# Hybrid attention block: weighted sums moved into the PSUM buffer of the step before, a narrower sum, and row sums by a column of ones

## The chip, the cores and the metric

The kernel runs on 1 core of one Trainium2 chip. The metric is the time on the device in microseconds (us). A run's time is that of one execution, and several runs are given by their median.

## The reference

One encoder layer over L = 16 meta tokens + 1024 frames of width 1024. RMSNorm, one input projection, two groups of eight heads, each head gated by a SiLU path, an output projection, RMSNorm and the residual. Cut to what matters here:

```python
for q0 in range(0, L, Q_BLOCK):                      # 128 queries at a time
    kend = key_end(q0)
    s = einsum('bqhd,bkhd->bhqk', q[:, q0:q0+Q_BLOCK], k[:, :kend]) * scale
    s = mask_and_bias(s, q0, kend)                   # causal + decay (FoX), chunk-causal (MLA)
    p = softmax(s, axis=-1)
    outs.append(einsum('bhqk,bkhd->bqhd', p, v[:, :kend]))
fox = ... * silu(f_gate); mla = ... * silu(m_gate)
y = concat([fox, mla]) @ w_out
return x + rmsnorm_post(y)
```

The head width is 64 in both groups. All products run in pairs of fp16 parts (a high part, and the rest as a low part), so that one product of the reference is three on the chip: high with high, high with low, low with high.

## The kernel before

**Stages.** A first stage normalises and transposes x and makes the latents and the values. Then come 16 heads, first 8 FoX heads and then 8 MLA heads, each of four steps; a tail finishes the output projection. A step treats a pair of query tiles, (7, 0), (6, 1), (5, 2) or (4, 3), so each step has nine key blocks of 128 and two short ones of 16 meta tokens: 1,184 columns of scores.

**One step n** (`step`):
- TensorE (PE): the scores of both tiles go into a PSUM buffer `sc` of three banks; there are two such buffers, used in turn. `places` leaves its first 256 columns free.
- VectorE (DVE): `peaks` takes two row maxima from PSUM, and one small operation makes the biases `nbs` (L806, L808).
- ScalarE (ACT): two exponentials from PSUM into `pr`, in f32 (L890). Each also sums its rows by `accum_out`, which costs a second instruction, the read of the accumulator.
- ACT writes the high fp16 part `ph` (L821); DVE subtracts to get the low part (L825), GpSimd (POOL) the part of the meta tokens (L902). This second half is emitted in the next step.
- A DMA transposes `ph` into `pT` (L905), which SyncE (SP) issues.
- Three steps after its scores (LAG = 3) a pair's weighted sums run on PE (`weighted`, L833 and L834), and DVE adds their two halves into `onat` (L918). They use the 256 free columns of the buffer that the step just then filled with its own scores.

`weighted` holds `pT` as the stationary operand, one load of weights for each product. The moving operand is `Vt`, whose high and low parts lie side by side: one product of 128 columns for the high part of the probabilities (11 in a step), one of 64 for their low part (9 in a step). The output of a tile is 128 columns wide.

**What orders the rest.** Between the steps `work` emits pieces of jobs: projections of the next heads (L960 to L962, L1174 to L1176, L1192 to L1194), and from the MLA heads on parts of the output projection (L1259 to L1261). Their results go through two one-bank buffers of `ps_g`. The framework tracks dependencies by PSUM bank and reorders each engine's instructions when the kernel is built, by when it expects them to be ready, so an engine's order in the trace need not be that of the code. On the chip each engine runs its own in that order.

**After a head.** `head_end` divides a head's rows by their sums (a reciprocal on DVE, a product on POOL); the last head does so pair by pair in `tiles_end`. In the tail the last three weighted sums use the third bank of the buffers that hold the output projection, `spare`.

Of the kernel before, what the change touches and what calls it, by code (L numbers as in the profile page):

```python
# [10 lines left out]
F32 = mybir.dt.float32  # L11
# [37 lines left out]
def hybrid_kernel(ctx, tc, x, meta, norm_pre, norm_post, w_in, b_f, q_norm, w_uq, kv_norm, w_ukv, w_out,  # L49
# [71 lines left out]
    Vt = V_pool.tile([P, NT + 1, H + 1, 2, HD], F16, name="Vt")  # L121
# [308 lines left out]
    def latents_V(t):  # L430
# [6 lines left out]
        split_v(pv, scale_mu, vm[:, :, 0, :], vm[:, :, 1, :])  # L437
        SY.dma_start(vm_d[:, :, t].rearrange("h p k d -> p h k d"), vm)

    def values_out(t, ps):  # L440
        split_v(ps, scale_fu, Vt[:, t, 1 : H + 1, 0, :], Vt[:, t, 1 : H + 1, 1, :])
# [333 lines left out]
    AVW = 2 * 2 * HD  # L775
# [60 lines left out]
    def head_end(onat, hh, sums):  # L836

        rs = at.tile([P, NT], F32, name="rs", tag="rs", bufs=2)
        V.reciprocal(rs, sums)
        o = onat[:, :, hh * HD : (hh + 1) * HD]  # L840
        G.tensor_tensor(o, o, rs.unsqueeze(2).to_broadcast([P, NT, HD]), ALU.mult)
# [31 lines left out]
    steps = {}  # L873

    def step(first, av=None):
# [3 lines left out]
        if first is not None:  # L879
            (ia, ib), passes, mask, mask_w, inv, sums = first[0:6]  # L880
            ps = step_psum("sc")
            av = ps[:, 0:AVW]
# [3 lines left out]
            pr = at.tile([P, wa + wb], F32, name="pr", tag="pr", bufs=2)  # L886
            prs = pr[:, 0:wa], pr[:, wa : wa + wb]
            for i, x, nb, p in reversed(list(zip((ia, ib), sc, nbs, prs))):

                A.activation(p, x, AF.Exp, bias=nb, scale=inv, accum_out=sums[:, i : i + 1])  # L890
# [3 lines left out]
            steps[n] = dict(t=(ia, ib), pr=prs, prw=pr, ph=ph, phs=(ph, ph[:, B0 * P :]), los=los, rest=first[6:])  # L894
# [17 lines left out]
        if old is not None:  # L912
            (ia, ib), pT = old["t"], old["pT"]
            vh, onat, hh, after = old["rest"]
            avs = av.rearrange("p (i t d) -> p i t d", i=2, t=2)
            weighted(avs[:, 1], ia, pT, pT[:, B0 + ib + 2 :, :], vh)
            weighted(avs[:, 0], ib, pT[:, B0:, :], pT[:, ia + 2 :, :], vh)
            V.tensor_reduce(onat[:, ib : ia + 1 : ia - ib, hh * HD : (hh + 1) * HD], avs.rearrange("p i t d -> p i d t"),  # L918
                            AX.X, ALU.add)
            if after is not None:  # L920
                after(ia, ib)

    def run_head(head, vh, hh, passes, mask, mask_w, inv, onat, after, each=None):

        sums = at.tile([P, NT], F32, name="sums", tag="sums", bufs=2)

        def end(ia, ib):
            head_end(onat, hh, sums)
# [4 lines left out]
        if each is not None:  # L933
            ends = [lambda ia, ib: each(ia, ib, sums)] * len(STEPS)

        total = sum(j[1] for j in jobs if j[0] == head)
        for k, tiles in enumerate(STEPS):
            step((tiles, passes, mask, mask_w, inv, sums, vh, onat, hh, ends[k]))
# [27 lines left out]
    def decays():  # L966
# [6 lines left out]
        V.tensor_tensor_scan(ncum[:, 0:NM], ones8f[0:H].to_broadcast([H, NM]), pf[0:H, 112:128], 0.0, ALU.mult, ALU.subtract)  # L973
        for t in range(1, NT + 1):
            T.transpose(pf[0:H, 512 + (t - 1) * P : 512 + t * P], lu[:, t, :], ident)
        V.tensor_tensor_scan(ncum[:, NM:L], ones8f[0:H].to_broadcast([H, S]), pf[0:H, 512:], ncum[:, NM - 1 : NM], ALU.mult, ALU.subtract)
# [243 lines left out]
    def load_values(h):  # L1220

        SY.dma_start(Vt[:, :, h], vm_d[h])
# [93 lines left out]
    ended = []  # L1316

    def tiles_end(ia, ib, sums):
        both = slice(ib, ia + 1, ia - ib)
        rs = at.tile([P, 2], F32, name="rs2", tag="rs2", bufs=2)  # L1320
        V.reciprocal(rs, sums[:, both])
        o = onat[:, both, HD:P]
# [180 lines left out]
```

## Time and profile before

| what | value |
| --- | --- |
| three runs | 628.46, 631.99, 632.98 us, median 631.99 |
| the profiled execution's own time | 630.43 us |
| its span | 628.6 us |
| mean granted clock of TensorE | 0.982 of full speed |
| PE busy | 558.2 us, 89% of the span |
| DVE busy | 478.2 us, 76% |
| ACT busy | 416.5 us, 66% |
| POOL busy | 198.8 us, 32% |

Matmuls are pipelined and the profile models their ends, so a busy PE need not be at its peak. "PEld" is the load of weights into TensorE, which runs beside the matmuls. "SPq" is SyncE's queue, from which the DMAs are issued. An idle time of an engine is put down to the instruction that ended it.

### The profile page before, as it was taken

How to read it: one execution, taken by the hardware profiler on the slowest of the kernel's cores; microseconds unless marked ns; L12 is line 12 of the kernel's file. 1: busy time of each engine (PE TensorE's matmuls, PEld its weight loads, DVE VectorE, ACT ScalarE, POOL GpSimd, SP SyncE). 2: the span in 40 equal slices, each digit the busy share in tenths (PEclk: the TensorE clock that was granted, in tenths of full speed). 3: DMA queues.
4: the chain of work that ended last, by engine and by line, in shares of the span. 5: the costliest groups of instructions: out<-in, count | busy, mean ns of one | idle time of the engine just before them, and what ended most of it. 6: DMA issues, size and time to landing. Idle time of an engine off the chain costs nothing.

```text
span 628.6 us, 11590 instructions
## 1 busy us (share of the span) xinstructions
PE 558.2 (89%) x4210; PEld 332.7 (53%) x4210; DVE 478.2 (76%) x953; ACT 416.5 (66%) x820; POOL 198.8 (32%) x282
## 2 busy tenths in 40 slices
PE   2999798989789999999999996988989989998994
PEld 1445354546346565656565553555555655655442
DVE  3778875576858787777797767889988887778667
ACT  5688868456867686656667657678677777686322
POOL 2223333373313233323343222123232313332242
PEclk9999899999999999999999998999999999999998
DMA  8858668165685987594858796697978868897943
GB/s 298 208 135 222 147 178 209 33 179 164 118 184 98 216 179 152 88 235 87 202 101 191 111 206 143 128 170 144 181 170 160 145 158 160 174 225 171 321 173 119
DMA packets 269529, 105.04 MB, mean 167 GB/s; under 512 B 234832, under 2 KB 257360, under 8 KB 269472
## 3 DMA queue, kind: packets, MB, share of 16 engines
q1 hardware_dynamic: 269472, 104.30, 73.5%
q8 instruction: 33, 0.54, 0.3%
q14 instruction: 24, 0.20, 0.1%
HBM read 48.38 MB, written 13.96 MB: 99 GB/s over the span
## 4 chain that ended last, share of the span: by engine, by line
DVE 31%; PE 27%; ACT 22%; issue 10%; DMA 5%; SPq 2%; POOL 1%; ACTq 0%; DVEq 0%; POOLq 0%
ACT pr L890 12%; DVE nb L806 9%; DVE ph L825 5%; ACT ph L821 4%; PE sc L834 3%; PE sc L796 2%; PE ps L306 2%; PE ps L304 2%; PE ps L305 2%; PE psf L1261 2%; PE psf L1259 2%; PE psf L1260 2%; DVE st L1053 2%; DMA wr<-in_w_in 2%; DMA wqr<-in_w_uq 1%
## 5 line engine op out<-in xcount | busy, mean ns | idle before, releaser
L825 DVE TENSOR_TENSOR ph<-pr,ph 128x128 f16<-128x128 f32 (+7 forms) x128 | 98.3, 778 | 30.8 <-ACT ph L821 30.2
L902 POOL TENSOR_TENSOR ph<-pr,ph 128x32 f16<-128x32 f32 x64 | 51.3, 802 | 222.1 <-issue 103.8
L806 DVE TENSOR_REDUCE nb<-sc 128x1 f32<-128x1040 f32 (+7 forms) x128 | 93.1, 766 | 5.6 <-PE sc L799 5.0
L890 ACT ACTIVATE pr<-sc,nbs,fox_inv 128x144 f32<-128x144 f32 (+3 forms) x64 | 53.5, 839 | 46.5 <-DVE nbs L808 41.4
L834 PE MATMUL sc<-Vt,pT 128*128 128x128 f16 x671 | 64.8, 222 | 20.2 <-ACT pr L890 19.4
L796 PE MATMUL sc<-st,st 128*128 128x256 f16 (+5 forms) x496 | 77.0, 291 | 2.2 <-ACT pr L890 1.3
L821 ACT CAST ph<-pr 128x912 f16<-128x912 f32 (+6 forms) x112 | 77.6, 737 | 0.2
L796 PEld LDWEIGHTS <-st 128*128 128x128 f16 x640 | 55.6, 98 | 29.7 <-issue 4.8
L833 PEld LDWEIGHTS <-pT 128*128 128x128 f16 x576 | 51.1, 99 | 35.1 <-issue 34.1
L890 ACT ACTIVATE pr<-sc,nbs,ism 128x144 f32<-128x144 f32 (+3 forms) x64 | 53.5, 840 | 24.3 <-DVE nbs L808 21.8
L834 PEld LDWEIGHTS <-pT 128*128 128x128 f16 x704 | 59.7, 99 | 6.1 <-issue 0.9
L833 PE MATMUL sc<-Vt,pT 128*128 128x64 f16 x549 | 57.9, 195 | 0.0
L960 PEld LDWEIGHTS <-wp 128*128 128x128 f16 x320 | 31.5, 98 | 30.1 <-DVE st L1054 4.9
L961 PEld LDWEIGHTS <-wp 128*128 128x128 f16 x320 | 31.5, 98 | 24.0 <-issue 4.1
L962 PEld LDWEIGHTS <-wp 128*128 128x128 f16 x320 | 31.5, 98 | 23.3 <-issue 0.8
L960 PE MATMUL psq<-xAh,wp 128*128 128x264 f16 x128 | 35.5, 277 | 1.0 <-DVE st L1054 1.0
L961 PE MATMUL psq<-xAl,wp 128*128 128x264 f16 x128 | 35.3, 276 | 0.0
L962 PE MATMUL psq<-xAh,wp 128*128 128x264 f16 x128 | 35.3, 276 | 0.0
L150 DVE SCALAR_TENSOR_TENSOR wp<-wr,bsc,wp 128x1024 f16<-128x1024 f32 x21 | 28.9, 1377 | 1.1 <-ACT wp L149 0.9
L960 PE MATMUL psg<-xBh,wp 128*128 128x512 f16 x64 | 25.1, 392 | 3.7 <-DVE kl L1201 3.2
L960 PE MATMUL psg<-xAh,wp 128*128 128x512 f16 x64 | 24.3, 379 | 2.8 <-DVE st L1054 2.8
L1259 PE MATMUL psf<-wo,xBh 128*128 128x512 f16 (+1 forms) x68 | 24.9, 366 | 1.1 <-DVE onatm L918 0.8
(370 smaller groups left out, 1466.7 us busy)
## 6 DMA issues: line engine op xcount, KB each, us to landing
wr<-in_w_in SPq DMA_DIRECT2D x20, 512.0 KB, 4.8
wr<-in_w_in SPq DMA_DIRECT2D x26, 256.0 KB, 3.9
wor<-in_w_out SPq DMA_DIRECT2D x8, 512.0 KB, 4.4
xr<-in_x SPq DMA_DIRECT2D x8, 512.0 KB, 5.7
xt<-in_x SPq DMA_DIRECT2D x7, 512.0 KB, 4.1
y_d<-ys SPq DMA_DIRECT2D x12, 256.0 KB, 2.3
y<-y_d SPq DMA_DIRECT2D x6, 512.0 KB
out<-y SPq DMA_DIRECT2D x5, 512.0 KB, 2.6
```

What stands on the lines that cost most here:

```text
L796: T.matmul(sc[:, o:o1], sta[:, i * P : (i + 1) * P], mov[:, o - c0 : o1 - c0], start=q == 0, stop=q == len(passes) - 1 and not last)
L806: V.tensor_reduce(nb[:, k : k + 1], part, AX.X, ALU.max, negate=True)
L821: A.copy(ph[:, 112 : 112 + W], pr)
L825: V.tensor_tensor(lo, pr[:, NM:W], ph[:, P : P + W - NM], ALU.subtract)
L833: T.matmul(avf[:, 0:HD], lo[:, j - 1, :], Vt[:, j, vh, 0], start=False, stop=False)
L834: T.matmul(avf, hi[:, j, :], Vt[:, j, vh].rearrange("p t d -> p (t d)"), start=j == 0, stop=j == n)
L890: A.activation(p, x, AF.Exp, bias=nb, scale=inv, accum_out=sums[:, i : i + 1])
L902: G.tensor_tensor(ph[:, 0 : B0 + 1 : B0, 96:112], n1[:, 0 : w0 + 1 : w0, :], ph[:, 0 : B0 + 1 : B0, 112:128], ALU.subtract)
L960: T.matmul(ps[:, 0:n], hi[:, c, :], xT(0, c, c0, n), start=c == 0, stop=False)
L961: T.matmul(ps[:, 0:n], hi[:, c, :], xT(1, c, c0, n), start=False, stop=False)
L962: T.matmul(ps[:, 0:n], lo[:, c, :], xT(0, c, c0, n), start=False, stop=c == NC - 1)
L1259: T.matmul(ps, hi, wh, start=c == first, stop=False)
```

## The change

1. The weighted sums of step n-3 are emitted right behind the scores of step n, and write the first 130 columns of the buffer `sc` of step n-1 (`older_step`, with `last`), no longer that of step n.
2. `Vt` gets rows of 130: low part (64), high part (64), two columns of ones. Each tile's sum is 65 columns wide: high and low probabilities times [high values | ones], 65 columns each (20 in a step), and high probabilities times low values, 64 columns (11 in a step). All add into the same 65 columns.
3. The column of ones gives the row sums, so the exponentials lose `accum_out`.
4. The DVE operation that added the two halves goes. ACT copies the 130 columns from PSUM to a new f32 tile `ona`; this copy is emitted between the step's two exponentials.
5. `head_end` and `tiles_end` read `ona` and write `onat`.
6. In the tail the last three sums use a buffer of `ps_g`; the Square root's table is loaded one step earlier; two transposes of a chain precede both products; a third step buffer takes the place of `spare` for the last tile; two f32 rows come from the pool `fw`.
7. In `decays` the eight transposes precede the first scan.

The diff, cut to its core:

```diff
-    Vt = V_pool.tile([P, NT + 1, H + 1, 2, HD], F16, name="Vt")
+    Vt = V_pool.tile([P, NT + 1, H + 1, 2 * HD + 2], F16, name="Vt")
+    G.memset(Vt[:, :, :, 2 * HD :], 1.0)
...
-        avf = av.rearrange("p t d -> p (t d)")
         for j in range(n + 1):
+            vl, v1 = Vt[:, j, vh, 0:HD], Vt[:, j, vh, HD : 2 * HD + 1]
+            T.matmul(av, hi[:, j, :], v1, start=j == 0, stop=False)
             if j > 0:
-                T.matmul(avf[:, 0:HD], lo[:, j - 1, :], Vt[:, j, vh, 0], start=False, stop=False)
-            T.matmul(avf, hi[:, j, :], Vt[:, j, vh].rearrange("p t d -> p (t d)"), start=j == 0, stop=j == n)
+                T.matmul(av, lo[:, j - 1, :], v1, start=False, stop=False)
+            T.matmul(av[:, 0:HD], hi[:, j, :], vl, start=False, stop=j == n)
...
+    def older_step(n, ps):
+        old = steps.get(n - LAG)
+        if old is None:
+            return
+        (ia, ib), pT = old["t"], old["pT"]
+        vh, ona, after = old["rest"]
+        av = ps[:, 0 : 2 * (HD + 1)].rearrange("p (i d) -> p i d", i=2)
+        weighted(av[:, 1], ia, pT, pT[:, B0 + ib + 2 :, :], vh)
+        weighted(av[:, 0], ib, pT[:, B0:, :], pT[:, ia + 2 :, :], vh)
+        A.copy(ona[:, ib : ia + 1 : ia - ib, :], av)
...
-            ps = step_psum("sc")
-            av = ps[:, 0:AVW]
+            last, psc[0] = psc[0], step_psum("sc")
+            ps = psc[0]
...
-                A.activation(p, x, AF.Exp, bias=nb, scale=inv, accum_out=sums[:, i : i + 1])
+            A.activation(prs[1], sc[1], AF.Exp, bias=nbs[1], scale=inv)
+            older_step(n, last)
+            A.activation(prs[0], sc[0], AF.Exp, bias=nbs[0], scale=inv)
...
+        else:
+            older_step(n, product("av"))
...
-            avs = av.rearrange("p (i t d) -> p i t d", i=2, t=2)
-            weighted(avs[:, 1], ia, pT, pT[:, B0 + ib + 2 :, :], vh)
-            weighted(avs[:, 0], ib, pT[:, B0:, :], pT[:, ia + 2 :, :], vh)
-            V.tensor_reduce(onat[:, ib : ia + 1 : ia - ib, hh * HD : (hh + 1) * HD], avs.rearrange("p i t d -> p i d t"),
-                            AX.X, ALU.add)
...
-        V.reciprocal(rs, sums)
+        V.reciprocal(rs, ona[:, :, HD])
...
-        SY.dma_start(Vt[:, :, h], vm_d[h])
+        SY.dma_start(Vt[:, :, h, 0 : 2 * HD], vm_d[h].rearrange("p t k d -> p t (k d)"))
...
-                            (spare[0][:, 0:256], 768, 256)]
+                            (step_psum("psf")[:, 0:256], 768, 256)]
```

## Rows read from the trace of the kernel before

**Rows 1.** Busy time by stage: the FoX heads, the MLA heads.

```profile
core 0: us, PE busy (x) PEld busy (x) DVE busy (x) ACT busy (x) POOL busy (x), PEclk, DMA share, GB/s
...
156.00:402.00 246.00, 223.04 (x1766) 138.21 (x1765) 183.99 (x316) 163.49 (x307) 71.89 (x92) 0.98 0.75 154
402.00:575.00 173.00, 155.86 (x1455) 98.60 (x1454) 149.09 (x279) 130.86 (x260) 52.32 (x54) 1.00 0.82 162
```

**Rows 2.** PE's waits, 156 to 402, then 402 to 575 us: total, times, longest.

```profile
PE sc L834 <- ACT pr L890: 12.5, 23, 2.9
...
PE sc L834 <- ACT pr L890: 6.8, 15, 1.2
...
PE psf L834 <- DVE onatm L918: 0.8, 1, 0.8
```

**Rows 3.** ACT, then PE, in one step of FoX: timeline (start, duration).

```profile
256.78 1.10 ACT L890 ACTIVATE pr<-sc,nbs,fox_inv 128x912 f32<-128x912 f32 x1
257.77 0.19 ACT L890 ACTIVATION_READ_ACCUMULATOR pr<-sc,nbs,fox_inv 128x1 f32 x1
...
258.02 0.22 PE L834 MATMUL sc<-Vt,pT 128*128 128x128 f16 x1 [0.74 <-ACT pr L890]
258.07 0.19 PE L833 MATMUL sc<-Vt,pT 128*128 128x64 f16 x1
258.10 0.22 PE L834 MATMUL sc<-Vt,pT 128*128 128x128 f16 x1
...
258.89 0.28 PE L961 MATMUL psq<-xAl,wp 128*128 128x264 f16 x1
```

**Rows 4.** Groups by line: busy us, mean ns, idle before.

```profile
L834 PEld LDWEIGHTS <-pT 128*128 128x128 f16 x704 | 59.7, 99 | 6.1 <-issue 0.9 <-DMA st<-lat_d 0.3
L918 DVE TENSOR_REDUCE onat<-sc 128x128 f32<-128x256 f32 x32 | 13.5, 421 | 8.2 <-PE sc L834 8.0
L890 ACT ACTIVATION_READ_ACCUMULATOR pr<-sc,nbs,ism 128x1 f32 x64 | 12.5, 196 | 0.0
```

**Rows 5.** Eight one-column products, each with a load of weights: PE timeline.

```profile
556.38 0.34 PE L1123 MATMUL wosum<-wo_sq,ones 128*128 128x1 bf16 x8
556.58 0.38 PE L1259 MATMUL psy<-wo,ogF 128*128 128x512 f16 x1
```

**Rows 6.** ACT copies of nearby size, by source line (ns min/median/max).

```profile
L142 ACT CAST xAh<-pt x10: 219/577/597, 11.7 to 53.2; 128x512 f16<-128x512 f32 x8, 128x64 f16<-128x64 f32 x2
L1166 ACT ACTIVATE wqh<-wqr,gqs x16: 385/400/412, 365.5 to 493.7; 128x128 f16<-128x128 f32 x16
```

**Rows 7.** A transpose's issue (SP), its pair's third-next scores' end (PE); landing times.

```profile
260.40 3.54 SPq L905 DMA_TRANSPOSE pT<-ph  x1
...
276.08 0.22 PE L799 MATMUL sc<-tri,ident 128*128 128x128 bf16 x1
...
429.50 3.08 SPq L905 DMA_TRANSPOSE pT<-ph  x1
...
433.46 0.19 PE L799 MATMUL sc<-blk,ident 128*128 128x64 bf16 x1
...
DMA to landing us min/median/max: 4.9/4.9/6.7
```

**Rows 8.** Two MLA steps in a bunch: PE's scores, ACT's first exponentials.

```profile
441.68 0.19 PE L799 MATMUL sc<-blk,ident 128*128 128x64 bf16 x1
...
442.36 1.33 PE L796 MATMUL sc<-st,st 128*128 128x256 f16 x9
...
443.90 0.19 PE L799 MATMUL sc<-blk,ident 128*128 128x64 bf16 x1
...
444.79 0.47 ACT L890 ACTIVATE pr<-sc,nbs,ism 128x144 f32<-128x144 f32 x1 [1.55 <-DVE nbs L808]
...
447.55 0.57 ACT L890 ACTIVATE pr<-sc,nbs,ism 128x272 f32<-128x272 f32 x1
```

**Rows 9.** Granted clock (PEclk) around the longest of these waits.

```profile
184.00:188.00 4.00, 1.71 (x21) 1.71 (x21) 0.53 (x2) 3.98 (x9) 0.76 (x2) 0.76 0.31 83
```

**Rows 10.** The second scan of `decays` on DVE and its wait: timeline.

```profile
133.00 2.33 DVE L976 TENSOR_TENSOR_SCAN ncum<-ones8f,ncum,pf 8x1024 f32<-8x1024 f32 x1 [1.26 <-PE pf L975]
```

More of the change, by code (lines that the diff above doesn't have):

```diff
@@ L774, in hybrid_kernel @@
     LAG = 3
-    AVW = 2 * 2 * HD
+    AVW = 256
     NPH = 3
@@ L873, in hybrid_kernel, with step @@
     steps = {}
-    def step(first, av=None):
+    last_pr = [None]
+    psc = [None]
+    def older_step(n, ps):
[8 more added lines that the diff above has]
+        A.copy(ona[:, ib : ia + 1 : ia - ib, :], av)
+    def step(first):
         now[0] += 1
@@ L879, in step @@
         if first is not None:
-            (ia, ib), passes, mask, mask_w, inv, sums = first[0:6]
-            ps = step_psum("sc")
-            av = ps[:, 0:AVW]
+            (ia, ib), passes, mask, mask_w, inv = first[0:5]
+            last, psc[0] = psc[0], step_psum("sc")
+            ps = psc[0]
             (a0, wa), (b0, wb) = places(ia, ib)
@@ L893, in step @@
             los = ph[:, la : la + (ia + 1) * P], ph[:, lb : lb + (ib + 1) * P]
-            steps[n] = dict(t=(ia, ib), pr=prs, prw=pr, ph=ph, phs=(ph, ph[:, B0 * P :]), los=los, rest=first[6:])
+            steps[n] = dict(t=(ia, ib), pr=prs, prw=pr, ph=ph, phs=(ph, ph[:, B0 * P :]), los=los, rest=first[5:])
+        else:
+            older_step(n, product("av"))
         evacuate()
@@ L923, in run_head @@
     def run_head(head, vh, hh, passes, mask, mask_w, inv, onat, after, each=None):
-        sums = at.tile([P, NT], F32, name="sums", tag="sums", bufs=2)
+        ona = at.tile([P, NT, HD + 1], F32, name="ona", tag="ona", bufs=2)
         def end(ia, ib):
-            head_end(onat, hh, sums)
+            head_end(onat, hh, ona)
             if after is not None:
@@ L933, in run_head @@
         if each is not None:
-            ends = [lambda ia, ib: each(ia, ib, sums)] * len(STEPS)
+            ends = [lambda ia, ib: each(ia, ib, ona)] * len(STEPS)
         total = sum(j[1] for j in jobs if j[0] == head)
         for k, tiles in enumerate(STEPS):
-            step((tiles, passes, mask, mask_w, inv, sums, vh, onat, hh, ends[k]))
+            step((tiles, passes, mask, mask_w, inv, vh, ona, ends[k]))
             work(head, 0.6 * total / len(STEPS))
@@ L1315, in hybrid_kernel, with tiles_end @@
     chains = deque()
-    ended = []
-    def tiles_end(ia, ib, sums):
+    def tiles_end(ia, ib, ona):
         both = slice(ib, ia + 1, ia - ib)
         rs = at.tile([P, 2], F32, name="rs2", tag="rs2", bufs=2)
-        V.reciprocal(rs, sums[:, both])
-        o = onat[:, both, HD:P]
-        V.tensor_tensor(o, o, rs.unsqueeze(2).to_broadcast([P, 2, HD]), ALU.mult)
-        ended.append(sums)
+        V.reciprocal(rs, ona[:, both, HD])
+        V.tensor_tensor(onat[:, both, HD:P], ona[:, both, 0:HD], rs.unsqueeze(2).to_broadcast([P, 2, HD]), ALU.mult)
         def chain():
@@ L1329, in chain @@
             for k, t in enumerate((ib, ia)):
+                T.transpose(ps[:, k * P : (k + 1) * P], onat[:, t, :], ident)
+            for k, t in enumerate((ib, ia)):
                 c = slice(k * P, (k + 1) * P)
-                T.transpose(ps[:, c], onat[:, t, :], ident)
                 V.scalar_tensor_tensor(og[:, c], ps[:, c], OUTK, gates[7, t // 4][:, t % 4 * P : (t % 4 + 1) * P],
@@ L1374, in hybrid_kernel @@
     rows = {}
-    slots = deque([(None, "row", 1), (at, "onat", 2)] + [(at, "pr", 2)] * 2 + [(at, f"ph{k}", 1) for k in range(NPH)]
-                  + [(at, "pT", 3)] * 3 + [(at, "onat", 2), (None, "row", 1)] + [(at, "pr", 2)] * 2 + [(at, f"ph{k}", 1) for k in range(NPH)])
+    slots = deque([(fw, "wh", 2), (at, "onat", 2)] + [(at, "pr", 2)] * 2 + [(at, f"ph{k}", 1) for k in range(NPH)]
+                  + [(at, "pT", 3)] * 3 + [(at, "onat", 2), (fw, "wh", 2)] + [(at, "pr", 2)] * 2 + [(at, f"ph{k}", 1) for k in range(NPH)])
     def row(name):
         pl, tag, bufs = slots.popleft()
-        if pl is None:
-            return fin.tile([P, D], F32, name=name, tag="row", bufs=1)
-        w = {"onat": D, "pr": 2 * NM + 9 * P}.get(tag, NBLK * P // 2)
+        w = {"onat": D, "wh": D, "pr": 2 * NM + 9 * P}.get(tag, NBLK * P // 2)
         return pl.tile([P, w], F32, name=name, tag=tag, bufs=bufs)[:, 0:D]
@@ L1439, in hybrid_kernel @@
     pss = {}
-    spare = [None]
     order = [t for pair in STEPS for t in pair]
-    load_late(order[0])
-    step(None, spare[0][:, 0:AVW])
-    load_late(order[1])
+    for t in order[:2]:
+        load_late(t)
+    step(None)
+    A.activation(warm, last_pr[0][:, 0:1], AF.Sqrt)
     for t in order[:3]:
@@ L1448, in hybrid_kernel @@
     products(order[0], 0, 7)
-    step(None, spare[0][:, 0:AVW])
-    A.activation(warm, ended[0][:, 3:4], AF.Sqrt)
+    step(None)
     chains.popleft()()
@@ L1459, in hybrid_kernel @@
         if k == 1:
-            step(None, spare[0][:, 0:AVW])
+            step(None)
         if k in (1, 3):
```

18 lines of the change are left out of this document (7 added, 11 removed).

## The prediction

> **What bounds the kernel now.** I read the table of stages first [rows 1]. In the FoX heads PE is busy for 223.0 of 246 us and in the MLA heads for 155.9 of 173, so PE does work or waits in a tenth of the time; no other engine comes near in the FoX stage (DVE 184, ACT 163), while in the MLA stage DVE follows closely with 149. What PE loses is then worth time, and what the others do less of is worth little unless PE waits for it. So the second view is PE's waits [rows 2]. The largest entry by far is that of the weighted sums (L834) for the exponentials (ACT L890): 12.5 us in 23 waits, then 6.8 us in 15, together 19.3 us of the 40.1 us (23.0 + 17.1) in which PE idles in the two stages. The third view shows what this wait is [rows 3]. The second exponential of a step and the read of its accumulator end at 257.96, and the first product of the weighted sums starts at 258.02. That product belongs to a pair three steps older and needs nothing of this step. It waits because its output lies in the bank that this step's exponentials still read. I compared all 64 steps: where the sums were not held up by something else, they start 0.14 us behind the end of the second exponential. In 26 steps other products fill PE until then, in 38 they do not.
>
> **The change part by part.** The sum is made against the profiled execution's own 630.43 us, whose span is 628.6; the three runs have a median of 631.99, so the profiled one is 1.6 us below it.
>
> *The wait goes.* In the new place the output shares a bank with the scores of the step before, whose exponentials ended long ago. The gain is at most the 19.3 us of [rows 2]. Two waits of 0.8 us in the tail's first step, for the DVE operation that is removed, go too (one has its row in [rows 2], that of L1259 is alike): -1.6 us, together -20.9. After the longest wait, of 2.9 us, the granted clock is 0.76 over 184 to 188 us [rows 9]: PE worked part of this stretch at 1.2 GHz in place of 2.4. Without the idle time before it I expect most of that back: 0.24 of 4 us is 1 us, I take -0.7, between 0 and -1.
>
> *The products.* Before, a step has 11 products of 128 columns and 9 of 64, in 0.87 us from 258.02 to 258.89 [rows 3]. A 64-column product takes 0.03 us there (258.07 to 258.10) and so does, within the rounding, (0.87 - 9 x 0.03) / 11 = 0.055 for one of 128. After, there are 20 of 65 columns and 11 of 64, each with its own load. At 0.029 each, 31 take 0.90 us, 0.03 more; over 64 steps +1.9 us, all on PE. The unknown is whether loads keep up when every product is short. Eight one-column products with their loads take 0.20 us [rows 5], 0.025 each, so the loads alone would allow 31 in 0.78 us: -6 us at that end. At the other end I let each product cost 0.033 (0.87 us less 11 x 0.0525, over 9): 1.02 us a step, +10. I take +1.9, since the row of 64 columns is the same product.
>
> The Trainium skill, "TensorE: Matmul & The Clock Gate", section "LDWEIGHTS (loading the stationary operand)", gives a load one nanosecond for each 1.2 columns, 107 ns for 128 columns. This speaks against a change that adds 11 loads a step: by it 31 loads would take 3.3 us and 20 now 2.1, 75 us more in 64 steps. The trace does not agree: twenty products with a load each pass in 0.87 us [rows 3].
>
> *DVE and ACT.* DVE loses 64 reductions of 0.42 us, 27 us in all, half of them in the MLA stage where it is the second bound [rows 1, 4]. ACT loses 128 reads of the accumulator of 0.196 us, 25 us [rows 4], of which about 0.1 each lies beside the exponential (the read starts at 257.77, the exponential runs to 257.88) [rows 3]. It gains 64 copies of 128 x 130 from PSUM. No such copy is shown: 0.22 us for 64 columns from PSUM, 0.40 for 128 with a factor from SBUF [rows 6]; I take 0.38, nearer to the second by its size: 24 us. At the ends ACT's sum is 64 x (0.22 - 0.39) = -11 us to 64 x (0.47 - 0.39) = +5, with the shortest exponential of [rows 8] as the upper price. ACT is busy for 131 of 173 us, so none of this is on PE's path by itself: 0.
>
> *Where the stall may go: the transposes.* The sums now want `pT` right at the end of the scores. In FoX there is room: issue at 260.40, scores three steps later at an end of 276.08 + 0.22, 15.9 us against a landing time of 4.9 [rows 7]. In MLA there is little: in the tightest step the issue is at 429.50 and the scores end at 433.65, 4.1 us. Of the 29 transposes of that stage one has less room than 4.9 us and eleven less than 6.7, the longest landing seen. If all land in 4.9, PE loses 1 us; if all take 6.7, 9 us. Behind the waiting product on PE stand the jobs, and on ACT the copy, with one or both exponentials behind it. I take +2, as the median landing is also the shortest.
>
> *Where the stall may go: the buffer.* The buffer of step n-1 is released only by the copy in step n, and the scores of n+1 wait for it. In the MLA stage two steps' scores run in a bunch (441.68, 442.36 to 444.09) [rows 8], and the second now has to wait for sums (0.9) and copy (0.4), 1.3 us and not 0.5. The framework orders by readiness: in [rows 8] the older sums of these steps have been put behind jobs. So I expect the copy ahead of the first exponential, which waits 2.9 us for the maxima (441.87 to 444.79), and jobs on PE meanwhile. Removing waits in a fixed order also makes PE meet others earlier: evacuations of the jobs, the next operands. I let a quarter of the 19.3 us return in these forms: +5, between 0 and +10.
>
> *The rest, with one answer each.* The wider rows of `Vt` change neither the transfers' count nor their bytes, and a head's values are loaded a head ahead: 0. The one memset runs on POOL while it waits for the first loads: 0. `head_end` has the same two operations: 0. In `decays` the second scan waits 1.26 us for PE [rows 10]; with the transposes first it can gain at most that: 0 to -1.3, I take 0, as the same transposes still come before it. In the tail the sums go from a spare bank to the two job buffers, which adds a wait or takes one: -2 to +2, 0 taken. SP's order changes nowhere else: no DMA is added, moved or removed.
>
> Sum: -20.9 - 0.7 + 1.9 + 2 + 5 = -12.7, that is 630.4 - 12.7 = 617.7 us.
>
> **Rivals.**
> A, *late transposes or copies eat the MLA gain.* For: the room of 4 to 7 us in a stage of 5.4 us a step [rows 1, 7]. Against: DVE is 13 us freer there and steps that no longer come in bunches have more room. At 9 us for the transposes in place of 2, and 10 returned in place of 5: 617.7 + 12 = about 630 with all of it, 626 with two thirds.
> B, *slower: the scores wait for the first exponential.* Its place is ACT's queue in the MLA stage, if the copy stands behind the first exponential. Then the scores of n+1 can start only when scores, maxima, exponential and copy of n are through. From [rows 8]: 441.87 to 445.26, plus 0.4, plus 1.7 for the scores is 5.5 us; for the second of the bunch 444.09 to 448.12, plus 2.1, is 6.1. Now a step has 173 / 32 = 5.4. At 6.1 in all 32 steps it costs 22 us, against a gain of 9 in FoX (12.5 + 0.7, less 1 for products and 3 returned): 643. Slower than now by over 1% takes 0.5 us in each MLA step. Against it: jobs can fill PE, and the copy is ready before the exponential.
> C, *it does not do what it says.* The framework puts the sums behind the jobs all the same, or another dependency holds them. Then the wait stays and the products come on top, while DVE's 27 us lie beside PE: 632.
> D, *loads set the pace.* If a short product behind a short product takes the 0.055 us of a wide one, 31 take 1.7 us: +53 us, 675 with the gains left at half. [Rows 5] speak against it. The Trainium skill's rule above is this case in a stronger form.
>
> **How the numbers follow.** Forecast 0.58 (617.7; alone 606 to 625), A 0.20, B 0.11, C 0.08, D 0.03. The low end of the range takes the products at their cheapest, nothing returned and the transposes in time: 630.4 - 21.9 - 6 + 1 = 603.5, I take 604. The high end takes in A and C and the first part of B: 634. Above it lie most of B and D, 0.12. About 1% is what a measurement of this kernel can tell from no change: 625.7 and 638.3 us around the median. Faster: 0.54 of the forecast and 0.08 of A, 0.62. Same: 0.04 of the forecast, 0.12 of A, C, and 0.02 of B, 0.26. Slower: 0.09 of B and D, 0.12.
>
> **What would show it.** Right: in the timeline the sums start within 0.2 us of the last mask product (L799) of each step's scores; the entry "L834 <- ACT pr L890" is gone from PE's waits; 31 products take 0.8 to 1.0 us; PE idles 25 us or so in the two stages. Wrong by A: a wait of the sums for a DMA, or a copy with ACT idle before it. Wrong by B: scores that wait for the copy. Wrong by C: jobs between scores and sums. The prediction fails most simply if PE's idle time stays at 40 us under other names.

## The result, and the profile after

The changed kernel takes 636.06 us (median of 13 runs, 633.20 to 638.86) against 631.27 (13 runs, 628.46 to 632.98): a ratio of 1.0079, with an interval of 1.0058 to 1.0099. It is slower by somewhat less than 1%, where 2.3% faster was forecast, and its median lies 2 us above the range. The profiled run took 633.20 us (span 631.0) and is the fastest of the 13, so its difference to the profile of before (span 628.6) shows only 2.4 us of the 4.8.

The stages come first, as in [rows 1].

```profile
core 0: us, PE busy (x) PEld busy (x) DVE busy (x) ACT busy (x) POOL busy (x), PEclk, DMA share, GB/s
156.00:402.00 246.00, 225.28 (x2147) 143.38 (x2145) 174.60 (x292) 167.64 (x279) 74.94 (x93) 0.98 0.78 157
402.00:575.00 173.00, 153.32 (x1731) 98.43 (x1727) 133.90 (x234) 125.78 (x217) 47.72 (x53) 0.97 0.79 155
```

PE idles 20.7 and 19.7 us in the two stretches, together 40.4, against 23.0 and 17.1, together 40.1, before [rows 1]. The prediction's part on what would show it named this as the simplest way to fail, and it is what happened: the idle time stayed, under other names. PE's waits say which, 156 to 402 us and then 402 to 575, to be held against [rows 2]:

```profile
engine line waited for: us in total, times, longest us
PE psg L973 <- DVE st L1067: 7.5, 5, 2.2
PE psk L1205 <- DVE qt L1193: 3.8, 1, 3.8
PE psq L973 <- DVE st L1067: 2.4, 2, 1.5
PE sc L834 <- ACT pr L907: 2.0, 3, 1.6
PE psq L973 <- DVE og L865: 2.0, 1, 2.0
...
PE sc L798 <- ACT ona L889: 8.9, 5, 2.7
PE sc L834 <- ACT pr L907: 6.7, 9, 1.5
PE sc L834 <- DMA pT<-ph: 2.5, 2, 1.4
```

In the FoX stage the wait of the sums for the exponentials fell from 12.5 us to 2.0. But the first product of a job (L973) waits 11.9 us in these rows for VectorE, which has to empty its bank, and 12.7 with two small entries more, where it waited 7.1 before (as L960); L1205 waits 3.8, before 1.6 (as L1192). Added up, PE's waits in this stretch are 22.5 us before and 20.9 after. In the MLA stage the wait for the exponentials stayed (6.8 before, 6.7 after), and scores that wait for ScalarE's copy came on top with 8.9.

To see where the span goes I took the end of the last mask product of the 6th, 33rd and 64th step from the timeline (L799 before, L801 after); a difference of two such ends is the length of a stage. Each is one run, and runs of one kernel differ by some 5 us.

```
us           to step 6   steps 6-33   steps 33-64   rest   span
before           189.4        210.6         167.6   60.9  628.6
after            185.8        211.0         175.2   59.0  631.0
after-before      -3.6         +0.4          +7.6   -1.9   +2.4
```

One step of FoX, PE's timeline (start, duration), answers [rows 3]:

```profile
233.91 0.22 PE L801 MATMUL sc<-tri,ident 128*128 128x128 bf16 x1
233.96 0.19 PE L834 MATMUL sc<-Vt,pT 128*128 128x65 f16 x1
...
234.89 0.38 PE L973 MATMUL psg<-xBh,wp 128*128 128x512 f16 x1
```

The sums start right behind the mask product, and the job's product follows 31 products later, after 0.93 us (233.96 to 234.89), measured as the 0.87 us of [rows 3] were. The groups by line, for [rows 4, 6]:

```profile
L827 DVE TENSOR_TENSOR ph<-pr,ph 128x512 f16<-128x512 f32 (+7 forms) x128 | 99.4, 782 | 67.7 <-ACT ph L823 66.7
...
L889 ACT COPY ona<-sc 128x130 f32<-128x130 f32 x61 | 16.3, 268 | 15.3 <-PE sc L837 14.4
```

ScalarE's copy takes 0.268 us. VectorE, rid of its 27 us of reductions, does not finish sooner: at L827 it waits 66.7 us for ScalarE's high parts, where it waited 30.2 before. The granted clock, for [rows 9]:

```profile
184.00:188.00 4.00, 4.00 (x61) 3.45 (x59) 1.67 (x3) 3.98 (x7) 1.10 (x1) 1.00 0.36 96
470.00:474.00 4.00, 4.00 (x16) 1.72 (x14) 3.35 (x7) 2.82 (x5) 1.16 (x1) 0.57 0.40 98
514.00:518.00 4.00, 2.05 (x8) 1.41 (x8) 2.43 (x5) 1.83 (x4) 0.24 (x1) 0.56 0.12 21
518.00:522.00 4.00, 4.00 (x16) 1.80 (x15) 2.77 (x6) 2.82 (x5) 1.16 (x1) 0.59 0.56 129
```

The fall to 1.2 GHz behind 184 us is gone, and two stretches at that level have come in the MLA stage, which had none before. In the FoX stage the falls have only moved: over 156 to 402 us the granted clock lacks 5.1 us of full speed before and after (added up in stretches of 2 us), after with a fall at 163 us, still in the first steps.

### The profile page after: what moved, and what is told of

It is laid out like the page before. It is cut to its first block, busy times and chain, and to the rows that moved or that the text cites. A ratio compares the mean times of both kernels' runs of the same rounds, so it can differ in the third digit from the quotient of the medians.

```text
span 631.0 us, 12856 instructions
## 1 busy us (share of the span) xinstructions
PE 559.9 (89%) x4914; PEld 339.2 (54%) x4914; DVE 455.5 (72%) x889; ACT 419.4 (66%) x756; POOL 197.5 (31%) x283
## 4 chain that ended last, share of the span: by engine, by line
DVE 19%; PE 18%; ACT 12%; issue 7%; DMA 7%; SPq 2%; POOL 0%; DVEq 0%; ACTq 0%; POOLq 0%
DVE nb L808 7%; ACT pr L907 4%; DMA pT<-ph 4%; ACT ph L823 4%; DVE ph L827 3%; PE sc L798 2%; PE psf L1274 2%; PE psf L1272 2%; PE psf L1273 2%; DVE nbs L810 1%; DMA wqr<-in_w_uq 1%; SPq L924 1%; PE psg L973 1%; PE psg L975 1%; PE psg L974 1%
## 5 line engine op out<-in xcount | busy, mean ns | idle before, releaser
L827 DVE TENSOR_TENSOR ph<-pr,ph 128x512 f16<-128x512 f32 (+7 forms) x128 | 99.4, 782 | 67.7 <-ACT ph L823 66.7
L921 POOL TENSOR_TENSOR ph<-pr,ph 128x32 f16<-128x32 f32 x64 | 53.1, 830 | 228.1 <-ACT ph L823 106.7
L823 ACT CAST ph<-pr 128x784 f16<-128x784 f32 (+6 forms) x112 | 78.0, 740 | 0.2
L834 PE MATMUL sc<-Vt,pT 128*128 128x65 f16 x671 | 64.7, 195 | 11.4 <-ACT pr L907 8.8
L837 PEld LDWEIGHTS <-pT 128*128 128x128 f16 x704 | 63.0, 99 | 11.6 <-issue 10.8
L837 PE MATMUL sc<-Vt,pT 128*128 128x64 f16 x671 | 66.5, 194 | 0.0
L834 PEld LDWEIGHTS <-pT 128*128 128x128 f16 x704 | 62.5, 98 | 7.2 <-DMA pT<-ph 4.8
L836 PE MATMUL sc<-Vt,pT 128*128 128x65 f16 x549 | 60.8, 195 | 0.0
L836 PEld LDWEIGHTS <-pT 128*128 128x128 f16 x576 | 53.6, 98 | 0.0
L973 PEld LDWEIGHTS <-wp 128*128 128x128 f16 x320 | 31.4, 98 | 34.3 <-DVE st L1067 12.2
L905 ACT ACTIVATE pr<-sc,nbs,fox_inv 128x144 f32<-128x144 f32 (+3 forms) x32 | 20.1, 629 | 43.3 <-DVE nbs L810 37.5
L973 PE MATMUL psq<-xAh,wp 128*128 128x264 f16 x128 | 35.6, 278 | 5.0 <-DVE st L1067 3.1
L905 ACT ACTIVATE pr<-sc,nbs,ism 128x144 f32<-128x144 f32 (+3 forms) x32 | 20.2, 631 | 23.1 <-DVE nbs L810 20.4
L907 ACT ACTIVATE pr<-sc,nbs,ism 128x1040 f32<-128x1040 f32 (+3 forms) x32 | 33.7, 1052 | 0.0
L907 ACT ACTIVATE pr<-sc,nbs,fox_inv 128x1040 f32<-128x1040 f32 (+3 forms) x32 | 33.6, 1051 | 0.0
```

What stands on the lines that cost most here:

```text
L823: A.copy(ph[:, 112 : 112 + W], pr)
L827: V.tensor_tensor(lo, pr[:, NM:W], ph[:, P : P + W - NM], ALU.subtract)
L834: T.matmul(av, hi[:, j, :], v1, start=j == 0, stop=False)
L836: T.matmul(av, lo[:, j - 1, :], v1, start=False, stop=False)
L837: T.matmul(av[:, 0:HD], hi[:, j, :], vl, start=False, stop=j == n)
L907: A.activation(prs[0], sc[0], AF.Exp, bias=nbs[0], scale=inv)
```

## The experiments

The expectations call the theories by letters. **P**: the shorter and more numerous products cost the time. **H**: the sums hold a step's buffer until the copy is through, and the next scores want it. **Q**: the copy heads ScalarE's queue while it waits for PE, and the exponential behind it starts late. **W**: what the removed wait gives PE is taken back at other waits, first of all those for the job banks that VectorE empties. **R**: the rival of W, as each expectation words it. Every kernel was timed beside the kernel before on the same chip, and the ratio is to that.

**The change by its parts.** e1 lets VectorE make the copy:

```diff
-        A.copy(ona[:, ib : ia + 1 : ia - ib, :], av)
+        V.tensor_copy(ona[:, ib : ia + 1 : ia - ib, :], av)
```

> The changed kernel with one operation moved: the copy of the 130 columns from PSUM runs on DVE and no longer on ACT. Theory H (the held buffer: the sum shares a bank with the exponentials of the step before, and the buffer comes free only with the copy, so the scores of two MLA steps can't run in a bunch): the copy still ends late and the time stays at 632 to 639 us, with PE's waits for the copy now put down to DVE. Rival Q (the copy stands at the head of ACT's queue, waits for PE, and so delays exponentials and high parts): 624 to 630 us, and DVE's wait for the high part falls from 66.7 us towards the 30.2 of before. Rival P (eleven more products and loads a step): no change, 636 us.

e2 has the new form of the sums, with the copy on ScalarE, in the old place (end of the step, in the step's own buffer):

```diff
-            older_step(n, last)
...
+        older_step(n, psc[0] if first is not None else product("av"))
```

> The new form of the sum alone, in the old place: three products in 65 columns, the column of ones and the copy on ACT, but behind the step's exponentials and in the step's own buffer. Theory H: the MLA loss of some 7 us goes, PE's wait for the exponentials (19 us) comes back: 626 to 634 us. Rival Q: a copy on ACT still stands in its queue, 634 to 640. Rival P: as slow as the changed kernel or slower, 636 to 642 us.

e3 has the old form (128 and 64 columns, `accum_out`, VectorE's reduction) in the new place:

```diff
-        A.copy(ona[:, ib : ia + 1 : ia - ib, :], av)
+        V.tensor_reduce(onat[:, ib : ia + 1 : ia - ib, hh * HD : (hh + 1) * HD], avs.rearrange("p i t d -> p i d t"),
+                        AX.X, ALU.add)
```

> The new place alone with the old form: products of 128 and 64 columns, accum_out in the exponentials, the two halves added on DVE, but right behind the scores and in the buffer of the step before. Theory H: as slow as the changed kernel or slower, since the buffer is held by an operation of DVE, the busier engine: 634 to 644 us, with scores that wait for that operation in the MLA stage. Rivals Q and P: nothing of the form is there, so the wait for the exponentials is gone for free: 615 to 626 us.

Measured: e1 629.21 us, ratio 0.9977 (0.9958 to 0.9996); e2 631.38, 1.0011 (0.9997 to 1.0026); e3 629.14, 0.9979 (0.9955 to 1.0002). The form costs nothing that can be told, so P falls, and so does the thought that a copy on ScalarE is dear by itself: in the old place it is free. e2 came out where H had it; e1 where Q had it (with VectorE's wait at L827 at 54.5 us, though, not near 30.2), and e3 where neither did. The place alone, with all else as before, removes most of the wait that the forecast was built on: of 19.3 us it leaves 1.0 in this window and 2.9 in the MLA stage. PE's waits, 156 to 402 us, of e3:

```profile
PE psg L972 <- DVE st L1066: 10.6, 6, 2.3
PE sc L796 <- DVE onat L887: 2.6, 2, 2.3
PE psq L972 <- DVE st L1066: 2.1, 2, 1.4
```

The entry for the exponentials is no longer at the top, and the kernel is only 1.5 us faster, with an interval that includes no change: the waits for the job banks (L1066) are 12.7 us, where they were 3.7 before (L1054). So the wait was never worth its length.

**Where the buffer and the copy stand.** e4 gives the sums a bank of the job buffers, so that they hold no scores' buffer:

```diff
-            older_step(n, last)
+            older_step(n, product("av"))
```

> The changed kernel with the sums in one of the two one-bank buffers of the jobs in place of the buffer of the step before: no bank is shared with exponentials, and the step buffers come free with the exponentials alone. Theory H: MLA's 8.9 us of scores waiting for the copy and 6.7 us of sums waiting for exponentials go, against waits of the jobs for a buffer: 622 to 632 us. Rivals Q and P: 634 us or more, as the copy still heads ACT's queue and the products are the same.

e5 holds the copy behind the step's second exponential in ScalarE's order; the sums on PE are not held:

```diff
-            older_step(n, last)
-            A.activation(prs[0], sc[0], AF.Exp, bias=nbs[0], scale=inv)
+            ex = A.activation(prs[0], sc[0], AF.Exp, bias=nbs[0], scale=inv)
+            with tc.issue_after(ex.ins):
+                older_step(n, last)
```

> The changed kernel with the ACT copy held behind the step's second exponential in ACT's order, where the framework had put it ahead of the first. Theory Q (the copy costs because it heads ACT's queue and waits there for PE's sums, 14.4 us in 15 waits): that wait goes, and the time falls by most of the 6.4 us that lie between a copy on ACT and one on DVE: 628 to 632 us. Rival H (the held buffer): the buffer comes free two exponentials later, scores wait longer for the copy: 640 us or more.

Measured: e4 642.56, 1.0203 (1.0183 to 1.0223); e5 660.72, 1.0473 (1.0455 to 1.0492). PE's waits of e4, 156 to 402 us:

```profile
PE av L834 <- DVE st L1067: 9.0, 7, 4.6
PE psq L973 <- DVE st L1067: 3.2, 2, 2.8
```

With a bank of their own the sums wait for VectorE themselves, so the job banks are the scarcer buffer: the FoX steps 6 to 33 take 225.0 us (211.0 in the changed kernel), and H's 622 to 632 is missed, though the MLA steps 33 to 64 are shorter (173.0, against 175.2). In e5 the copy waits for PE only in the tail, and the MLA steps take 197.9 us where they took 175.2. A later release of the buffer thus costs far more than the copy's wait for PE, as H has it. It does not show that this wait costs nothing: e1 and e4 came out where Q had them, and no run takes it away without moving the release too.

**Stage by stage.** e6 uses the new place in the FoX heads only, e7 in the MLA heads only, both with VectorE's copy (e6; e7 has `blk` for `tri`):

```diff
-            older_step(n, last)
+            if mask is tri:
+                older_step(n, last)
...
+        if first is not None and not (mask is tri):
+            older_step(n, psc[0])
```

> The copy on DVE as in the first experiment; the new place only in the FoX heads, the old one (behind the exponentials, in the step's own buffer) in the MLA heads. Theory H for the MLA stage (the held buffer costs a few us there): 621 to 627 us. Theory W (what a removed wait gives back on PE returns at other waits of PE, so neither place matters by itself): 628 to 632 us.

> The copy on DVE; the new place only in the MLA heads, the old one in the FoX heads. Theory H: 632 to 638 us. Theory W: 628 to 632 us, the same as with the places exchanged.

Measured: e6 633.08, 1.0023 (1.0007 to 1.0038); e7 635.61, 1.0081 (1.0056 to 1.0105). e7 came out where H had it and e6 where neither did; W's 628 to 632 held for neither. The parts don't add up to e1, which has both: by themselves they give +0.2% and +0.8%, together -0.2%. A change of place alters the order on all engines, at the seam too; I draw nothing from this pair.

**What takes the FoX gain back.** This is what W looks like, PE, DVE and ACT of the changed kernel, 222 to 228 us:

```profile
225.68 0.19 PE L837 MATMUL sc<-Vt,pT 128*128 128x64 f16 x1
227.65 0.39 PE L973 MATMUL psg<-xAh,wp 128*128 128x512 f16 x1 [1.79 <-DVE st L1067]
...
225.49 1.09 DVE L827 TENSOR_TENSOR ph<-pr,ph 128x896 f16<-128x896 f32 x1 [0.42 <-ACT ph L823]
226.62 0.47 DVE L1066 SCALAR_TENSOR_TENSOR st<-psq,fox_c,st 64x248 f16<-64x248 f32 x1
227.10 0.50 DVE L1067 SCALAR_TENSOR_TENSOR st<-psq,fox_c,st 64x264 f16<-64x264 f32 x1
...
222.72 0.58 ACT L905 ACTIVATE pr<-sc,nbs,fox_inv 128x272 f32<-128x272 f32 x1 [2.29 <-DVE nbs L810]
223.20 1.10 ACT L907 ACTIVATE pr<-sc,nbs,fox_inv 128x912 f32<-128x912 f32 x1
224.19 1.27 ACT L823 CAST ph<-pr 128x272 f16<-128x272 f32 x2
```

PE is through with the sums at 225.87. Its next job needs a bank that L1066 and L1067 empty; they stand on VectorE behind the low part L827, which waited for the high part L823, which stood behind the exponentials. With the order of ScalarE and VectorE as it is here, PE in the old place would have waited for the exponentials (they end at 224.30), then run the products (0.87 us, to 225.3), and it would still have met this bank ahead of 227.60. Where two waits follow one another and the second ends at an event that the first does not move, taking the first away only lengthens the second. That is argued from one timeline. In the kernel before, the same step runs otherwise (VectorE and PE):

```profile
226.07 0.50 DVE L1054 SCALAR_TENSOR_TENSOR st<-psq,fox_c,st 64x264 f16<-64x264 f32 x1
226.81 0.22 PE L834 MATMUL sc<-Vt,pT 128*128 128x128 f16 x1 [0.54 <-ACT pr L890]
228.08 0.38 PE L960 MATMUL psg<-xAh,wp 128*128 128x512 f16 x1
```

There the bank is empty at 226.57, before the exponentials end (226.67), and the job's product does not wait. So the release itself comes later in the changed kernel, 3.3 us behind the exponentials' end, as the two operations stand behind the low parts. The next runs test whether they are what stands in the way.

Five kernels change that chain. e8 (the kernel before) and e9 (e1) leave out the 48 VectorE operations; e15 does the same to the changed kernel:

```diff
-                    V.scalar_tensor_tensor(QS[64:128, qs], pq, cq, QS[0:64, qs], ALU.mult, ALU.subtract)
-                    V.scalar_tensor_tensor(K2[0:64, ks], pk, ckk, KS[0:64, ks], ALU.mult, ALU.subtract)
+                    return
```

> The kernel before, without the low parts of the FoX queries and keys: 48 VectorE operations of about 0.57 us (L1053 and L1054), 27 us, that stand between the job products and the release of their PSUM banks, are left out, and zeros stand in their place; PE's work is the same. It is half of a pair with e9. Theory W (what the new place saves on PE is taken back by waits for the job banks, which VectorE empties behind its low parts): these operations are on PE's path already now, so this kernel is 3 to 10 us faster than before. Rival R (the FoX step has another loop that sets its length, from scores over maxima, exponentials and copies, and the job banks only fill the time): under 2 us faster.

> The new place with VectorE's copy (e1), without the same 48 operations. W: with fewer operations ahead of the banks the new place keeps more of its 19 us, so this kernel is at least 6 us faster than e8, where e1 was 1.4 us faster than before. R: the difference to e8 stays at 0 to 3 us.

> The changed kernel without the 48 VectorE operations for the low parts of the FoX queries and keys, as in e8 and e9 (zeros stand in their place). W: 6 to 12 us faster than the changed kernel, 624 to 630, all of it before the MLA stage, whose steps 33 to 64 keep about 175 us where e9 has 171. Rival (only a copy on VectorE can use the room): 634 to 637.

Measured: e8 631.84, 1.0010 (0.9987 to 1.0033); e9 618.99, 0.9801 (0.9753 to 0.9849); e15 626.01, 0.9944 (0.9923 to 0.9965). In the old place 27 us of VectorE's work cost nothing; there W's expectation failed and R's held, since the wait for the exponentials covers the banks: with the waits for L1054 gone it is 15.9 us, where it was 12.5. In the new place they cost 1.8% on top of e1 and 1.4% on top of the changed kernel: e9 is 12.9 us faster than e8, and e15 is at 626.0 us, both where W had them. PE's waits of e9, 156 to 402 us:

```profile
PE psq L973 <- ACT st L1062: 5.0, 2, 4.5
PE sc L798 <- DVE ona L889: 4.6, 4, 1.6
PE psq L973 <- DVE og L865: 2.5, 1, 2.5
```

They add up to 15.7 us there, 22.8 in e8. The steps 6 to 33 take 206.3 us in e9 and 207.6 in e15, against 213.5 in e8; 33 to 64 take 171.3 in e9 and 178.1 in e15. Of e15's gain in the profiles (631.0 to 625.7 us) 4.9 us lie ahead of step 6 and 3.4 in these FoX steps. So the FoX gain is there once VectorE does not stand in its way, and the loss in MLA stays with the changed kernel.

e10 (the kernel before) and e11 (e1) leave out the low parts of the probabilities instead, which stand ahead of the banks in VectorE's queue:

```diff
-            for i, p, h, l in zip(prev["t"], prev["pr"], prev["phs"], prev["los"]):
-                low(i, p, h, l)
```

> The kernel before, without VectorE's low parts of the probabilities (L825, 128 operations, 98 us, and with them VectorE's wait of 30 us for ScalarE's high parts); the products that use them run on what stands there, so PE, ScalarE and the transposes have the same work. Half of a pair with e11. W: VectorE no longer holds anything up, the waits for job banks go: 5 to 15 us faster than before. R: under 3 us faster.

> e1 (new place, VectorE's copy) without the same low parts. W: the new place now keeps most of its gain, so this kernel is 8 to 20 us faster than e10. R: the difference to e10 stays at 0 to 3 us, as what sets the step's length is neither the wait that went nor VectorE's queue.

Measured: e10 624.23, 0.9892 (0.9843 to 0.9942); e11 619.86, 0.9822 (0.9786 to 0.9858). The difference of 4.4 us lies between what W (8 to 20) and R (0 to 3) expected. The FoX steps 6 to 33 stay at 210.1 and 211.2 us: with the low parts gone, VectorE waits in front of the same 48 operations for ScalarE's high parts of the job. DVE's waits of e11, 190 to 395 us:

```profile
DVE st L1064 <- ACT st L1059: 39.6, 11, 7.4
DVE ge L1090 <- ACT ge L1083: 16.3, 6, 3.7
```

So in FoX it is not VectorE's low parts that make the step long, but the chain over ScalarE. What both kernels gain lies in the MLA stage: the steps 33 to 64 take 160.4 us in e10 and 162.9 in e11, where before and e1 take 167.6 and 169.8.

**Bank or queue?** e12 (the kernel before), e13 (e1) and e14 (the changed kernel) empty the job banks by one ScalarE operation into SBUF and leave no work out:

```diff
-                A.activation(QS[0:64, qs], pq, AF.Copy, scale=cq)
-                A.activation(KS[0:64, ks], pk, AF.Copy, scale=ckk)
+                A.activation(sq[:, 0:n], ps[:, 0:n], AF.Copy, scale=fox_c[:, h : h + 1])
+                ...
+                G.tensor_copy(QS[0:64, qs], sq)
+                G.tensor_copy(KS[64:128, ks], sk)
...
-                    V.scalar_tensor_tensor(QS[64:128, qs], pq, cq, QS[0:64, qs], ALU.mult, ALU.subtract)
+                    V.tensor_tensor(QS[64:128, qs], sq, QS[0:64, qs], ALU.subtract)
```

> The kernel before, with all its work, but the job banks of the FoX projections are emptied by one ScalarE operation of 128 partitions into SBUF (24 in place of 48, some 11 us less on ScalarE); the high parts are made from there by GpSimd and the low parts by VectorE, so the bank no longer waits for VectorE. Control for e13. Theory W and its rival both expect within 1% of before, as leaving VectorE's half out changed nothing (e8).

> e1 (new place, VectorE's copy) with the same way to empty the job banks, no work left out. W (the new place's gain in FoX is taken back by waits for the job banks behind VectorE's queue): 5 to 12 us faster than e12, and the FoX steps 6 to 33 take under 208 us, where before and e1 take 211 to 212. Rival (e9 was faster because VectorE had 27 us less to do, not because the banks came free): 0 to 3 us faster than e12, FoX steps at 211 us.

> The changed kernel itself (copy on ScalarE) with the same way to empty the job banks. W: gains in FoX as e13 does, 3 to 8 us, and stays 4 to 6 us behind e13, since its MLA stage is the same as before this edit. Rival: no change, 636.

Measured: e12 645.33, 1.0250 (1.0213 to 1.0287); e13 642.52, 1.0206 (1.0174 to 1.0238); e14 648.30, 1.0291 (1.0252 to 1.0329). All are 2.1 to 2.5% slower than the kernels that they are made from, for a reason of their own. DVE's waits of e12, 156 to 402 us:

```profile
DVE st L1057 <- POOL st L1051: 17.8, 9, 5.2
DVE st L1058 <- POOL st L1052: 4.9, 12, 0.5
```

VectorE now waits 22.7 us for GpSimd, and e12, which was to be within 1% of before, is not; so the three say nothing about the banks. e16 (the kernel before), e17 (e1) and e18 (the changed kernel) keep the 48 operations and their waits, and let them read SBUF in place of the bank:

```diff
-                    V.scalar_tensor_tensor(QS[64:128, qs], pq, cq, QS[0:64, qs], ALU.mult, ALU.subtract)
-                    V.scalar_tensor_tensor(K2[0:64, ks], pk, ckk, KS[0:64, ks], ALU.mult, ALU.subtract)
+                    V.scalar_tensor_tensor(QS[64:128, qs], QS[0:64, qs], cq, QS[0:64, qs], ALU.mult, ALU.subtract)
+                    V.scalar_tensor_tensor(K2[0:64, ks], KS[0:64, ks], cq, KS[0:64, ks], ALU.mult, ALU.subtract)
```

> The kernel before with the 48 VectorE operations for the low parts of the FoX queries and keys in place, but both of their operands come from SBUF (the high parts stand in for the PSUM values, so the low parts are not those of the reference). They wait for ScalarE's high parts as before; the job bank comes free once ScalarE has read it. Control for the next two. Both theories: 629 to 633, as leaving them out altogether changed nothing in the old place (e8).

> e1 with the same edit. If what takes the gain back is the release of the job banks behind VectorE's queue: 617 to 623, as in e9, and 8 to 14 us faster than e16; the FoX steps 6 to 33 take 206 to 208 us. If it is VectorE's time or the order of its queue: 627 to 631, as e1, at most 3 us faster than e16, steps 6 to 33 at 211 to 213 us.

> The changed kernel with the same edit. Release of the banks: 624 to 629, as in e15, with FoX steps 6 to 33 at about 207.5 us. VectorE's time or order: 634 to 638, steps at 211 us.

Measured: e16 632.68, 1.0037 (1.0016 to 1.0059); e17 624.48, 0.9905 (0.9871 to 0.9940); e18 637.21, 1.0117 (1.0078 to 1.0156). With VectorE's copy the free bank is worth 0.7% over e1, or 1.3% over its control e16: part of what e9 gained, though the operations have become slower (0.75 us in the mean of e17's 34 between 190 and 395 us, 0.56 in e1). Its FoX steps 6 to 33 take 209.9 us, between the two expectations; in the control e16 they take 216.9, 6.3 more than before. With ScalarE's copy the free bank brings nothing: the steps take 216.8 us in e18, 211.0 in the changed kernel. PE's waits of e18, 156 to 402 us:

```profile
PE sc L834 <- ACT pr L907: 8.3, 5, 2.3
PE psk L1205 <- DVE qt L1193: 3.8, 1, 3.8
PE psq L973 <- DVE og L865: 3.1, 2, 2.9
```

The banks' entry for L1067 is gone here too, and the time stands at the sums' wait for the exponentials again (8.3 us, 2.0 in the changed kernel). For e1 the release of the banks is shown as a part of what took the gain. For the changed kernel it is shown that these operations stand in its way (e15). e18 does not clear the bank, as its operations are slower too (0.73 us in the mean, 0.56 in the changed kernel) and could take back what a free bank gives. Whether it is the bank, their time or their place in VectorE's queue stays open there.

**The MLA stage.** One step of the changed kernel before the second fall of the clock, PE and ACT:

```profile
511.20 0.19 PE L801 MATMUL sc<-blk,ident 128*128 128x64 bf16 x1
512.87 0.19 PE L834 MATMUL sc<-Vt,pT 128*128 128x65 f16 x1 [1.48 <-ACT pr L907]
...
515.95 0.46 PE L798 MATMUL sc<-st,st 128*128 128x368 f16 x1 [1.99 <-ACT ona L889]
...
511.61 1.21 ACT L907 ACTIVATE pr<-sc,nbs,ism 128x1040 f32<-128x1040 f32 x1
...
514.50 0.55 ACT L1210 ACTIVATE kh<-psk,cmk 64x346 f16<-64x346 f32 x1
515.06 0.55 ACT L1210 ACTIVATE st<-psk,cmk 64x346 f16<-64x346 f32 x1
515.63 0.27 ACT L889 COPY ona<-sc 128x130 f32<-128x130 f32 x1
```

The scores end at 511.39, the sums wait 1.48 us for an exponential of the step before, whose buffer they share. They end at 513.96, and the copy starts 1.67 us later, behind a high part (L823) and work for a job (L1210) in ScalarE's order; the next scores wait 1.99 us for it. Over the next 8 us the granted clock is 0.56 and 0.59, that is 1.2 GHz for most of it. In stretches of 2 us I added up what the granted clock lacks: 5.1 us in the MLA stage (402 to 575) of the changed kernel, none before, and none in e1, whose steps 33 to 64 take 169.8 us. In all kernels with ScalarE's copy in the new place and the usual order (the changed one, e14, e15, e18) these steps take 175 to 178 us; with VectorE's copy (e1, e9, e13, e17) 170 to 171, and 172.3 in e7; in the old place (before, e2, e8, e12, e16) 168 to 169. Two kernels do not fit: e3, with VectorE's reduction in the new place, has 175.2, and e6, with VectorE's copy in the old place, 172.0. Nor is the clock all of the loss: within these steps it lacks 5.1 us in e15, whose steps take 10.5 us more than those of e8, where it lacks nothing.

## Why the prediction was wrong

**The step that failed.** The first term, "The wait goes", with its reason that the output shares a bank with scores "whose exponentials ended long ago", and the term against it, "I let a quarter of the 19.3 us return in these forms". The first half holds in FoX, not in MLA, where 9 waits with 6.7 us are left: scores come in bunches, and the exponentials of the step before have then not ended. The second half was mis-sized. Of the 19.3 us, 2.9 (the longest wait of [rows 2]) lay in the first steps and were gained. The other 9.6 of FoX gave nothing: the steps 6 to 33 take 210.6 us before and 211.0 after. The 6.8 of MLA became a loss of 7.6. In place of a quarter, the whole returned in the steady steps.

**What the runs showed in its place.** The wait stood in series with others that end later, and PE met those instead. In FoX these are the job banks, behind a chain of exponentials and high parts on ScalarE and the 48 operations on VectorE (e8, e9, e15); without the low parts of the probabilities the steps are hardly shorter (e11: 211.2 us, e1: 212.4). The text had them as "evacuations of the jobs" in a sentence, and priced them by a share of the wait instead of asking, at each wait, when the next thing that PE needs would be ready. In MLA it is the buffer's release by the copy, which the text named too ("1.3 us and not 0.5"); in the steps shown PE waits 2 us for it each time, and the lower clock about these waits lacks 5.1 us. Rival B put the loss in that place, at 22 us over the kernel before, with the copy behind the first exponential; the copy was behind job work instead. With it behind both exponentials (e5) the steps 33 to 64 take 22.7 us more than in the changed kernel and 30.3 more than before.

**What held.** The products: 0.93 us for 31, 0.90 forecast, and e2 shows the form free. By an estimate from the Trainium skill, "TensorE: Matmul & The Clock Gate", section "LDWEIGHTS (loading the stationary operand)", 31 loads of 128 columns would have taken 3.3 us. The trace does not agree here either. The late transposes: 2.5 us in the MLA stage, 2 forecast. The tail: 1.9 us shorter, 1.6 forecast. The clock around 184 us is back at full, but the 0.7 us set for it are not shown: the fall came at 163 us instead. The scan in `decays`: it waits no longer and starts at 132.49 in place of 133.00, with nothing to show for it later. ScalarE's copy: 0.268 us, below the 0.38 that I took. That VectorE's 27 us would be worth nothing by themselves: L827 waits 36.5 us longer for ScalarE.

**What stays open.** In the new place ScalarE's copy is 1.0% slower than VectorE's (1.0079 and 0.9977). The MLA steps and their clock are where the profiles differ, but profiles are single runs, and why ScalarE comes to the copy late was only read from one timeline. e6 and e7 do not add up. Every edit also lets the framework order all engines anew, and no run held that order fixed; an effect of the order alone, of the size of the changed kernel's 0.8%, is not excluded. The fastest kernel that leaves nothing out is e1, at 0.9977 (e3 is the same within the intervals).

## What to carry to other kernels

A wait in the table of waits has a price only if nothing that ends later stands behind it on the same engine: before taking one as a gain, follow the engine to its next two needs, and write down when each is ready by a chain that the wait does not touch. Here the place alone (e3) removed 15 us of the 19 and saved 1.5. Where a result is parked in a buffer that the next step wants, its copy out belongs on the engine that reaches it first, here VectorE (e1), and a short idle time there can be followed by a stretch at the lower clock: about two waits of 2 us in the MLA stage it lacked 1.7 and 3.4 us.

## What the runs showed of the hardware that I had not expected

A fall of TensorE's granted clock lacked 1.7 us of full speed in most cases. Between 156 and 575 us the changed kernel has five stretches at 1.2 GHz in place of 2.4; by the granted clock four of them lack 1.7 us of full speed and the one from 514 us 3.4. The four that I followed, from 250 us on, lie about waits of PE of 2 to 4 us.

The sums write columns 0 to 129 of a buffer whose scores start at column 256, yet they wait for the exponentials that read those scores (6.7 us in MLA). The Trainium skill, "PSUM — Partial Sum Buffer", section "PSUM bank collisions raise a hardware error", has it that accesses of two engines must be kept apart by bank and group of 32 partitions, and not by address. The trace agrees in so far as the wait is there, and in e4, where the sums have a bank of their own, no wait of theirs for an exponential shows.

VectorE's operation on 64 partitions became slower, 0.56 to 0.75 us in the mean, when its operands were f16 in SBUF in place of f32 in PSUM and f16 in SBUF (e1 and e17). It is not slower by itself: those of e17 with no GpSimd instruction beside them took 0.48 us for 264 columns and 0.73 for 512 (a single one), where e1 has 0.49 and 0.75 throughout. Beside GpSimd's instructions they took up to 1.17 and 1.74 us, and those of e1, with one operand in PSUM, did not slow down there.
